# A product-key expert layer in a two-layer diffusion backbone: 75 instead of 80 dense classes, 56 instead of 50 gathered slots per token, nine instead of eight rounds of eight picks

## The chip, the cores and the metric

The kernel runs on one core of a Trainium2 chip, as one program. The metric is device time in microseconds (us) for one execution, from the chip's own profiler or from timed runs; lower is better. Engines are named as in the profile: PE is the matrix engine, PEld its weight loads, DVE the vector engine, ACT the scalar engine, POOL the engine that issues the gathers, SP the one that issues the ordinary loads.

## The reference

A backbone of two layers over 256 tokens of width 1024. Layer 0 mixes with state-space heads and latent attention, layer 1 with a gated MLP. After either mixer comes the part that the change concerns, an expert layer with product keys:

```python
s1 = einsum('thd,hkd->thk', q[..., :half], k1); s2 = einsum('thd,hkd->thk', q[..., half:], k2)
v1, i1 = top_k(s1, 16);  v2, i2 = top_k(s2, 16)               # 8 heads, 128 keys each
top_s, j = top_k(v1 + v2 over all pairs, 16)                  # 16 experts of 16384 per head
gate = softmax(top_s)
act = gelu(einsum('phkd,pd->phk', u_tab[idx], t))             # rows of the u table
out = einsum('phk,phkd->pd', gate * act, v_tab[idx])          # rows of the v table
```

So each token picks 8 x 16 = 128 experts, and each expert is a row of 1024 numbers in the u table and one in the v table, in float32.

## The kernel before

An expert (i1, i2) belongs to class (i1 + i2) mod 128; each of the 128 classes has 128 experts. Classes 0 to X-1 are computed densely, for all 256 tokens, whether they were picked or not. Experts picked from classes X to 127 are gathered, row by row.

**Dense classes.** `products()` issues the PE's work. For each class of a first pass ("S"), eight float32 products of the u weights (a 512 KB load, `in_dn` to a `wr` buffer; there are four) with the tokens `phf` give scores in a `pa` bank; ACT applies gelu and the result lands in row c of the tile `ge`. For each class of a second pass ("V"), eight products of `ge` with the v weights (again 512 KB) accumulate in four `pb` banks, `py`. A float32 product is two records in the profile, so one class is 16 records in either pass.

**Spread.** Between the passes `ge` has to be multiplied with the gates. `spread()` does so in 32 blocks of eight tokens: DVE builds one-hot tiles `o1`, `eq` and `oc` by comparison (their widths hold X), PE multiplies them (16 records of 128x80), DVE and ACT apply the result. The V pass starts when all blocks are done.

**Own slots.** `gather()` works through CAP slots for each of two tiles of 128 tokens (t = 0, 1). A slot holds one gathered expert for each of the 128 tokens: POOL issues one indirect transfer of up to 128 rows of 8 KB (u and v side by side, from `in_uv`) to one of NR = 6 `rows` buffers, DVE takes the dot product with the tokens (`junk<-rows,h`), ACT applies gelu and gate, DVE adds the weighted row to `acc`. A token that has no more picks carries an index out of bounds there, and its row isn't moved. Between t = 0 and t = 1 `acc` is stored (`acs<-acc`) and used again. The indices come out of `take8()`, one round of eight largest keys per call: MAX8, MATCH_REPLACE8, some small operations and eight `mk` operations. There are ROUNDS rounds for each t. Those that the slots of t = 0 and t = 1 don't need at once are drawn one by one in the iterations of t = 1 from its fifth slot on.

**The shared list.** Picks in places CAP to 8 * ROUNDS - 1 go to a list that all tokens share, with room for SHARED * 128 = 384. `listing()` builds it (DVE counts, `cnt`, and small products on PE). Its three slots are gathered last, each with a second gather of the tokens (`rows<-hs`), and DVE makes a tile `sc` of weights; PE then adds them to the same `py` banks (`pb<-rows,sc`, 24 records for three slots). If more picks are left over than the list holds, a branch `overflow()` works them off at the end.

**Order.** Each engine works through its own queue in the order in which the program was written. That order comes from `schedule()`, a planner that runs at build time with its own clocks: it always takes the stream whose engine is least far. Its costs are 3.42 for a class on PE, 2.93 for a row transfer and 1.49 for a class load on one clock "D" for all transfers. `gather()` is held back by a pace:

```python
rest = len(todo) - head[0] + len(work)
nxt[0] = max(nxt[0], clk["T"] - 3.0) + PACE * PTILE * max(0, left[0] - TAIL) / max(1, rest)
if rest:
    yield lambda: clk["T"] > nxt[0] and not urgent()
```

`left` counts the dense classes still to come (both passes), PTILE is 3.5 and TAIL is 10. When the list's `sc` is ready by the planner's clock, its products are written into PE's queue at the place that PE has reached by then; the classes that come later stand behind them. After the last class `update()` adds `py` and `acc` to the stream `x`.

All groups of the profile carry the line 169, that of a helper which every operation passes through, so they are told apart by tiles.

Of the kernel before, what the change touches and what calls it, by code (L numbers as in the profile page):

```python
# [23 lines left out]
EPS = 1e-6  # L24
NEG = -3.0e38

X = 80
GSC = 32768.0
ROOM = 36
TB, TL = 8, 4  # L30
CAP = 50
ROUNDS = 8
SHARED = 3
NR = 6
PRI = {}
# [162 lines left out]
def tile_backbone(ctx: ExitStack, tc: tile.TileContext, a: dict, out: bass.AP):  # L198
# [102 lines left out]
    ms = [dp.tile([P, 512], F32, name=f"ms{g}") for g in (1, 2)]  # L301
    LEFT = 8 * ROUNDS - CAP
    lts = dp.tile([2 * P * LEFT, 2], F32, name="lts")
# [93 lines left out]

    PEER = [(w, c_) for w in "SV" for c_ in range(X)]
    feed = Feed()
# [198 lines left out]
    def hybrid(mod):  # L598
# [444 lines left out]
        def scores():  # L1043
            for p_ in range(4):
# [40 lines left out]
                for h in range(2):  # L1085
                    b0 = 64 * h
                    for t in range(2):
# [4 lines left out]
                        mx = h2.tile([P, 1], F32, tag="mx", name="mx", bufs=4)  # L1092
                        V.tensor_reduce(mx, ps, axis=AX.X, op=ALU.max)
                        V.tensor_scalar(mx, mx, -scale, None, op0=ALU.mult)
# [196 lines left out]
    def gmlp(mod, a1, sh1):  # L1291
# [29 lines left out]
        def centre(t):  # L1321
            mu = gw.tile([P, 1], F32, tag="mu", name="mu")
            V.reduce_sum(mu, sums[t], axis=AX.X)
            V.tensor_scalar(mu, mu, 1.0 / 2048, None, op0=ALU.mult)
            V.tensor_scalar(v[t], v[t], mu, None, op0=ALU.subtract)
            for hf in range(2):
                junk, vh = gw.tile([P, D], F32, tag="xw", name="junk"), v[t][:, hf * D:(hf + 1) * D]
                V.scalar_tensor_tensor(junk, vh, 1.0, vh, op0=ALU.mult, op1=ALU.mult, accum_out=lss[t][:, hf:hf + 1])
            V.reduce_sum(lr[:, t:t + 1], lss[t], axis=AX.X)

# [82 lines left out]
    def peer(l, mod, a2, sh2):  # L1413
# [22 lines left out]
        hh = q1.tile([P, KD, 256], F32R, name="phh", tag="phh")  # L1436
        ge = q1.tile([P, X, 256], F32, name="ge")
        pkT = [q1.tile([P, 4, P], F16, name=f"pkT{t}") for t in range(2)]
        gidx = [q1.tile([P, 8 * ROUNDS], I32, name=f"gidx{t}") for t in range(2)]
        gsel = [q1.tile([P, 8 * ROUNDS], F32, name=f"gsel{t}") for t in range(2)]  # L1440
        gte = [q1.tile([P, P], F32, name=f"gte{t}") for t in range(2)]
# [3 lines left out]
        xb, g2 = spare[1:3], spare[3]  # L1445
        left = [2 * X]
        done = set()
# [150 lines left out]
        def take8(t, r_, idx=None, gsl=None):  # L1598

            if idx is None:  # L1600
                idx, gsl = gidx[t][:, 8 * r_:8 * r_ + 8], gsel[t][:, 8 * r_:8 * r_ + 8]
            ks = q2.tile([P, 8], F32, tag="ks", name="ks")
            V.max(ks, key[t][r_ % 2])
            V.match_replace(key[t][(r_ + 1) % 2], ks, key[t][r_ % 2], 0.0)
            ki = q2.tile([P, 8], I32, tag="ki", name="ki")
            V.tensor_copy(ki, ks)
            z_ = q2.tile([P, 8], F32, tag="z_", name="z_")
            V.tensor_scalar(z_, ks, 0.0, 65536.0, op0=ALU.is_equal, op1=ALU.mult)
            V.tensor_scalar(idx, ki, 8, None, op0=ALU.logical_shift_right)
            V.tensor_tensor(idx, idx, z_, op=ALU.add)  # L1610
            V.tensor_scalar(ki, ki, 255, None, op0=ALU.bitwise_and)
            j1 = q2.tile([P, 8], F32, tag="j1", name="j1")
            V.tensor_copy(j1, ki)
            for s_ in range(8):
                mk = q2.tile([P, P], F32, tag="mk", name="mk")
                V.scalar_tensor_tensor(mk, jp1, j1[:, s_:s_ + 1], gte[t], op0=ALU.is_equal, op1=ALU.mult, accum_out=gsl[:, s_:s_ + 1])
# [192 lines left out]
        def listing():  # L1809
# [4 lines left out]
            for t in range(2):  # L1814
                vm = q2.tile([P, LEFT], F32, tag="vm", name="vm")
                V.tensor_scalar(vm, gidx[t][:, CAP:], 65536.0, None, op0=ALU.is_lt)
                V.reduce_sum(cnt[:, t:t + 1], vm, axis=AX.X)
                V.tensor_copy(rhs[:, t, 1:2], cnt[:, t:t + 1])
                gl = q2.tile([P, LEFT, 2], F32, tag="gl", name="gl")
                V.tensor_copy(gl[:, :, 0], gidx[t][:, CAP:])  # L1820
                V.tensor_copy(gl[:, :, 1], gsel[t][:, CAP:])
                S.dma_start(out=lts[t * P * LEFT:(t + 1) * P * LEFT, :].rearrange("(p j) c -> p (j c)", j=LEFT), in_=gl.rearrange("p j c -> p (j c)"))
                fl = q2.tile([P, 1], F32, tag="fl", name="fl")
                V.tensor_reduce(fl, key[t][ROUNDS % 2], axis=AX.X, op=ALU.max)
                V.tensor_scalar(fl, fl, 0.0, None, op0=ALU.is_gt)
# [36 lines left out]
        def gather():  # L1862
            yield lambda: "sel" in done
            nxt = [clk["T"]]
            todo = [(t, s) for t in range(2) for s in range(CAP)] + [(2, k) for k in range(SHARED)]
            free, work, pend = list(qr["rows"]), [], []
# [31 lines left out]
            def accumulate():  # L1898
# [11 lines left out]
                else:  # L1910
                    V.scalar_tensor_tensor(acc[1], v_, w, acc[1], op0=ALU.mult, op1=ALU.add)
                if t == 0 and s == CAP - 1:
                    Q.dma_start(out=acs, in_=acc[1])
# [7 lines left out]
            while work or pend:  # L1921
                weigh_last()
                if work:
# [6 lines left out]
                    if t == 1 and s >= 4:  # L1930

                        if taken[0] < ROUNDS or taken[1] < ROUNDS:
                            t_ = 0 if taken[0] < ROUNDS else 1
                            take8(t_, taken[t_])
# [196 lines left out]
```

## Time and profile before

| what | value |
|---|---|
| timed runs, median of 3 (lowest to highest) | 2077.2 us (2073.23 to 2078.44) |
| the profiled execution | 2073.34 us, of it span 2071.6 us |
| PE busy | 1945.0 us, 94% of the span |
| DVE busy | 1368.5 us, 66% |
| POOL busy | 592.2 us, 29% |
| HBM read | 525.60 MB, 257 GB/s over the span |
| first V class on PE, layer 0 | 865.0 us |
| first V class on PE, layer 1 | 1747.5 us |

The span is counted from the first to the last instruction; the windows below are us from its start. A busy engine isn't an engine at its peak: a product that waits inside PE's pipeline still counts as busy.

### The profile page before, as it was taken

How to read it: one execution, taken by the hardware profiler on the slowest of the kernel's cores; microseconds unless marked ns; L12 is line 12 of the kernel's file. 1: busy time of each engine (PE TensorE's matmuls, PEld its weight loads, DVE VectorE, ACT ScalarE, POOL GpSimd, SP SyncE). 2: the span in 40 equal slices, each digit the busy share in tenths (PEclk: the TensorE clock that was granted, in tenths of full speed). 3: DMA queues.
4: the chain of work that ended last, by engine and by line, in shares of the span. 5: the costliest groups of instructions: out<-in, count | busy, mean ns of one | idle time of the engine just before them, and what ended most of it. 6: DMA issues, size and time to landing. Idle time of an engine off the chain costs nothing.

```text
span 2071.6 us, 28401 instructions
## 1 busy us (share of the span) xinstructions
PE 1945.0 (94%) x10048; PEld 1574.3 (76%) x10048; DVE 1368.5 (66%) x3634; ACT 540.4 (26%) x1386; POOL 592.2 (29%) x378
## 2 busy tenths in 40 slices
PE   7899999999989999998999998999899999989997
PEld 4565444579878888887877788789688888878786
DVE  3575566247988678878664226579888887776651
ACT  4434343344212122210111154442122221101100
POOL 1324222166011112223221188550111112233210
PEclk9999999999989999999999999999999999989999
DMA  8556664555468668998997364454678788989972
GB/s 302 171 184 215 212 217 145 165 173 184 133 225 293 237 220 310 379 378 293 417 410 260 132 234 153 156 191 128 229 283 307 269 297 298 365 295 412 413 274 82
DMA packets 132489, 519.98 MB, mean 251 GB/s; under 512 B 17222, under 2 KB 17414, under 8 KB 107179
## 3 DMA queue, kind: packets, MB, share of 16 engines
q1 hardware_dynamic: 100320, 312.24, 43.2%
q0 software_dynamic: 30720, 204.69, 25.9%
q8 instruction: 79, 1.29, 0.2%
q10 hardware_dynamic: 1296, 1.15, 0.2%
q14 instruction: 74, 0.61, 0.1%
HBM read 525.60 MB, written 6.91 MB: 257 GB/s over the span
## 4 chain that ended last, share of the span: by engine, by line
PE 55%; DVE 19%; issue 12%; DMA 7%; POOL 5%; ACT 2%; POOLq 0%; SPq 0%; ACTq 0%; DVEq 0%
PE pb L169 28%; PE pa L169 27%; DVE ge L169 6%; DMA wr<-in_dn 4%; POOL rows L169 2%; DVE mk L169 2%; POOL whl L169 2%; DVE acc L169 1%; DVE junk L169 1%; DMA acs<-acc 1%; DVE rows L169 1%; DMA rows<-in_uv,gidx 1%; DVE x L169 1%; DVE oc L169 1%; DVE cacc L169 0%
## 5 line engine op out<-in xcount | busy, mean ns | idle before, releaser
L169 PE MATMUL pa<-phf,wr 128*128 128x256 f32 x2560 | 576.1, 386 | 0.0
L169 PE MATMUL pb<-wr,ge 128*128 128x256 f32 x2560 | 569.4, 383 | 6.5 <-DMA wr<-in_dn 5.4
L169 PEld LDWEIGHTS pb<-wr,ge 128*128 128x128 f32 x2560 | 485.2, 191 | 90.3 <-DMA wr<-in_dn 22.9
L169 PEld LDWEIGHTS pa<-phf,wr 128*128 128x128 f32 x2560 | 492.3, 194 | 67.2
L169 POOL DMA_INDIRECT rows<-in_uv,gidx x200 | 231.7, 1158 | 916.8 <-DVE acc L169 608.0
L169 POOL TENSOR_TENSOR whl<-wr,whl 128x1024 fp32r<-128x1024 f32 (+2 forms) x130 | 314.7, 2434 | 401.9 <-ACT whl L169 392.2
L169 DVE SCALAR_TENSOR_TENSOR junk<-rows,h 128x1024 bf16<-128x1024 f32 x200 | 244.0, 1220 | 85.6 <-DMA rows<-in_uv,gidx 82.5
L169 DVE SCALAR_TENSOR_TENSOR acc<-rows,wt,acc 128x1024 f32<-128x1024 f32 x196 | 250.7, 1279 | 0.0
L169 ACT ACTIVATE act<-act 128x1 f32<-128x1 f32 x206 | 41.7, 203 | 435.6 <-DVE junk L169 420.6
L169 ACT CAST whl<-wr 128x1024 fp32r<-128x1024 f32 (+2 forms) x136 | 136.9, 1018 | 70.7 <-PE pa L169 27.7
L169 ACT ACTIVATE sg<-pa 128x256 f32<-128x256 f32 (+25 forms) x126 | 38.8, 308 | 383.9 <-PE pa L169 375.4
L169 PE MATMUL pb<-oc,o 128*128 128x80 f16 x1024 | 88.2, 255 | 31.8 <-DVE oc L169 31.8
L169 PEld LDWEIGHTS <-o 128*128 128x128 f16 x1024 | 80.8, 118 | 40.9 <-DVE o L169 16.3
L169 PE MATMUL pa<-phh,whl 128*128 128x256 f32 x512 | 96.3, 285 | 2.1 <-DVE phf L169 2.1
L169 PE MATMUL pb<-aw,condT 128*32 128x512 f32 x328 | 93.4, 624 | 5.1 <-DVE mod L169 3.0
L169 DVE SCALAR_TENSOR_TENSOR ge<-pb,ge 128x80 f32<-128x80 f32 (+29 forms) x128 | 36.9, 316 | 78.3 <-ACT ge L169 77.2
L169 PEld LDWEIGHTS pa<-phh,whl 128*128 128x128 f32 x512 | 80.8, 191 | 4.0 <-DVE phf L169 2.5
L169 PE MATMUL pa<-phl,whl 128*128 128x256 f32 x256 | 73.2, 286 | 2.4 <-POOL phl L169 1.3
L169 DVE SCALAR_TENSOR_TENSOR mk<-jp,j,gte 128x128 f32<-128x128 f32 x256 | 72.4, 347 | 1.1
L169 PE MATMUL pb<-whl,cath 128*128 128x512 f32 x192 | 61.8, 400 | 2.0 <-POOL whl L169 1.1
L169 ACT ACTIVATE wt<-act,gsel 128x1 f32<-128x1 f32 x200 | 58.9, 295 | 6.5
L169 DVE TENSOR_TENSOR oc<-eq,pkT 128x640 f16<-128x640 f16 x128 | 57.1, 487 | 2.2
(517 smaller groups left out, 2402.0 us busy)
## 6 DMA issues: line engine op xcount, KB each, us to landing
wr<-in_dn SPq DMA_DIRECT2D x320, 512.0 KB
aw<-in_ada_w SPq DMA_DIRECT2D x164, 256.0 KB
wr<-in_wq SPq DMA_DIRECT2D x32, 512.0 KB
wr<-in_w_out SPq DMA_DIRECT2D x16, 512.0 KB
wr<-in_gm_w_v SPq DMA_DIRECT2D x16, 512.0 KB
wr<-in_gm_w_u SPq DMA_DIRECT2D x16, 512.0 KB
wr<-in_gm_w_out SPq DMA_DIRECT2D x16, 512.0 KB
wr<-in_w_xbc SPq DMA_DIRECT2D x12, 512.0 KB
```

What stands on the lines that cost most here:

```text
L169: return f(*args, **kw)
```

## The change

Three constants. X sets how many classes are dense, and with it the length of both passes, the size of `ge`, the width of the spread's tiles and the split of the tables in memory. CAP is the number of own slots per token tile; ROUNDS is the number of calls of `take8()` per token tile. The room for the list's candidates per token, 8 * ROUNDS - CAP, goes from 14 to 16.

```diff
-X = 80
+X = 75
 GSC = 32768.0
 ROOM = 36
 TB, TL = 8, 4
-CAP = 50
-ROUNDS = 8
+CAP = 56
+ROUNDS = 9
 SHARED = 3
 NR = 6
```

## Rows read from the trace of the kernel before

**Rows 1.** From the page: the span; the gathers' queue (packets, MB, share).
```profile
span 2071.6 us, 28401 instructions
...
q0 software_dynamic: 30720, 204.69, 25.9%
```

**Rows 2.** Windows by stage: us, busy by engine (instructions), PE clock, DMA share, GB/s.
```profile
606.00:864.00 258.00, 250.44 (x1425) 220.61 (x1423) 200.30 (x472) 54.01 (x239) 41.60 (x40) 0.97 0.77 281
864.00:960.00 96.00, 86.08 (x397) 74.32 (x395) 83.58 (x319) 11.08 (x43) 28.42 (x19) 0.97 0.92 352
960.00:1000.00 40.00, 40.00 (x187) 35.46 (x186) 26.34 (x53) 4.97 (x20) 17.00 (x13) 0.93 0.89 329
1000.00:1100.00 100.00, 98.39 (x438) 81.23 (x437) 67.13 (x84) 13.93 (x56) 26.69 (x27) 1.00 1.00 404
...
1121.00:1176.00 55.00, 55.00 (x250) 43.68 (x249) 5.14 (x11) 4.29 (x9) 0.00 (x0) 1.00 0.37 124
...
1490.00:1754.00 264.00, 255.34 (x1487) 226.20 (x1488) 217.48 (x518) 57.63 (x260) 47.82 (x45) 0.97 0.82 297
...
1876.00:1976.00 100.00, 97.78 (x429) 79.25 (x428) 64.08 (x81) 12.93 (x52) 25.70 (x26) 1.00 1.01 410
```

**Rows 3.** Timeline of PE, end of layer 0: start, us, what.
```profile
1099.77 30.38 PE L169 MATMUL pb<-wr,ge 128*128 128x256 f32 x140
1129.99 10.46 PE L169 MATMUL pb<-rows,sc 128*128 128x512 f32 x24
1140.29 34.70 PE L169 MATMUL pb<-wr,ge 128*128 128x256 f32 x160
```

**Rows 4.** Timeline of DVE, end of layer 0; in brackets idle time before it.
```profile
1109.08 0.41 DVE L169 TENSOR_SCALAR sc<-iotaL,spot,wt 128x256 f32<-128x256 f32 x1
...
1120.84 0.08 DVE L169 DVE_READ_ACCUMULATOR junk<-rows,rows 128x1 f32 x1
1133.70 0.41 DVE L169 TENSOR_SCALAR sc<-iotaL,spot,wt 128x256 f32<-128x256 f32 x1 [12.78 <-PE pb L169]
...
1170.71 0.69 DVE L169 TENSOR_TENSOR x<-pb,ge 128x512 f32<-128x512 f32 x1 [36.30 <-PE pb L169]
```

**Rows 5.** Timeline of PE, end of layer 1.
```profile
2015.09 10.46 PE L169 MATMUL pb<-rows,sc 128*128 128x512 f32 x24
2025.39 34.70 PE L169 MATMUL pb<-wr,ge 128*128 128x256 f32 x160
```

**Rows 6.** Timeline of DVE, end of layer 1.
```profile
2006.29 0.08 DVE L169 DVE_READ_ACCUMULATOR junk<-rows,rows 128x1 f32 x1
```

**Rows 7.** Groups of 1000 to 1100: count, busy us, mean ns, idle before it.
```profile
L169 PE MATMUL pb<-wr,ge 128*128 128x256 f32 x438 | 99.0, 383 | 1.6 <-DMA wr<-in_dn 1.1
...
L169 DVE SCALAR_TENSOR_TENSOR acc<-rows,wt,acc 128x1024 f32<-128x1024 f32 x28 | 35.8, 1279 | 0.0
L169 DVE SCALAR_TENSOR_TENSOR junk<-rows,h 128x1024 bf16<-128x1024 f32 x28 | 34.3, 1225 | 34.2 <-DMA rows<-in_uv,gidx 34.2
```

**Rows 8.** The chain that ended last, 960 to 1060: start, us, what.
```profile
968.76 41.56 PE pb L169 x192
...
1036.84 3.72 PE pb L169 x16
```

**Rows 9.** Timeline of PE, the building of the list in layer 0.
```profile
959.45 0.56 PE L169 MATMUL pa<-cnt,tri 128*128 128x1 f32 x2 [7.45 <-DVE cnt L169]
```

**Rows 10.** Groups of 606 to 864, the S stage of layer 0.
```profile
L169 DVE SCALAR_TENSOR_TENSOR junk<-rows,h 128x1024 bf16<-128x1024 f32 x43 | 52.4, 1218 | 0.0
...
L169 DVE TENSOR_TENSOR oc<-eq,pkT 128x640 f16<-128x640 f16 x60 | 26.8, 487 | 1.0
```

**Rows 11.** Timeline of DVE: the first row is the first of a round of picks.
```profile
909.99 0.28 DVE L169 MAX8 ks<-key 128x8 f32<-128x128 f32 x1
...
913.81 1.28 DVE L169 SCALAR_TENSOR_TENSOR acc<-rows,wt,acc 128x1024 f32<-128x1024 f32 x1
```

**Rows 12.** Transfers of 864 to 1120.
```profile
DMA packets 19562, 94.40 MB, mean 369 GB/s; under 512 B 3268, under 2 KB 3268, under 8 KB 12835
```

## The prediction, made before the change was run

> **What bounds the kernel now.** I read the windows by stage first, then the ends of both layers on PE and DVE, then the saturated stretch in between. In the S stage (606 to 864) PE is busy 250 of 258 us, DVE 200, the transfers 77% [rows 2]: PE sets the pace. In the V stage the transfers fill up: 404 GB/s at a share of 1.00 from 1000 to 1100, 410 in layer 1 [rows 2]; there DVE waits 34.2 of 100 us for gathered rows [rows 7], and PE's classes come every 100 / (438 / 16) = 3.65 us [rows 7] instead of 41.56 / 12 = 3.46 [rows 8]. So after 864 the gathers run at the transfers' limit and PE just behind its own.
>
> The reader should look longest at the end of a layer. PE meets the list's products at 1129.99, and behind them stand 160 records, ten classes, 34.70 us [rows 3]; layer 1 is the same [rows 5]. DVE has the list ready just before: first `sc` at 1109.08, third dot product finished at 1120.84 (layer 1: 2006.29); its third `sc` then waits 12.78 us only because PE hasn't used the first [rows 4, 6]. After that DVE idles 36.30 us for PE [rows 4]. The 55 us from 1121 on with transfers at 37% [rows 2] look like ample cover for more gathers. They aren't: PE works its queue in order, and a list that comes after PE has reached its place holds back every class behind it. The true slack is 1130 - 1121 = 9 us, and this decides the change.
>
> **What the change removes.** Five S and five V classes in each layer: 10 x 3.46 = 34.6 us of PE a layer, 69.2 in all [rows 8]. Were PE alone the bound, that would be the gain. The one-hot tiles get 6% narrower: `oc` takes 487 ns for 640 elements [rows 10], and if all of it scaled, 64 of them would save 2 us of DVE a layer; bounds 0 and 5 with `eq` and the applying; it falls into the S stage, where DVE idles 58 of 258 us [rows 2], so I take 0. PE's spread products get narrower as well; 0 too.
>
> **What it adds.** Two layers of two tiles get six more own slots: 24 gathers, 12 a layer, each 1.225 + 1.279 = 2.50 us of DVE [rows 7], 30 us a layer. Two more rounds of picks a layer at 913.81 - 909.99 = 3.82 us [rows 11]: 7.6. They come in the burst behind the store of `acc`, where DVE is busy 83.6 of 96 us [rows 2] and nothing hides them: everything behind them on DVE's queue, the building of the list and all later slots, moves by 7.6.
>
> Transfers: I counted the reference's own picks for these inputs. Classes from 80 on get 48.3 and 48.0 picks a token in the two layers, from 75 on 53.3 and 53.0. Own slots then move 13335 rows instead of 11978 in layer 0 (13332 and 11990 in layer 1), the list 306 instead of 376 (230 and 301). In bytes up to the list's end: +1357 x 8192 = 11.1 MB, -70 x 12288 = -0.9, and ten class loads fewer at 0.524, -5.2: together +5.0 MB. (By this count the old gathers move (11978 + 11990) x 8192 + 677 x 12288 = 204.7 MB, which the page's queue shows [rows 1].) At the V stage's mean of 369 GB/s [rows 12] 5.0 MB are 13.6 us.
>
> So the list is ready later than before, in absolute time, by 0 us if the S stage takes all of it (23% of its transfer time is idle [rows 2]), by 12 x 100 / 28 = 42.9 plus 7.6 = 50 us if each new slot costs what a slot costs in the saturated stretch [rows 7]. I take the bytes and the picks, 13.6 + 7.6 = 21.2: the stage behind S is limited by bytes most of the time [rows 2], the burst by DVE. That the S stage ends 17 us sooner gives the gathers nothing: they are ordered by the same queue and filled its holes before.
>
> The Trainium skill's page "DMA: Bandwidth & Descriptors" (Specifications) gives about 358 GB/s as the limit of one core's memory traffic. The rows contradict it here, with 404 and 410 [rows 2]. By it the 107 MB of the new V stage (94.4 [rows 12], 13 more gathers of 0.98 there) would need 299 us from 848, the list would come at 1148 and not at 1142, and the total would be some 12 us higher.
>
> **Where the list stands in PE's queue.** The planner deals out about one gather per class in V: its transfer clock is full with 2.93 + 1.49 = 4.42 per pair, more than PE's 3.42. Before, 43 of the first 50 slots are done by 864 [rows 10]: 57 own and 3 list slots are left, the eight rounds of picks cost it some ten more classes, and it ends with ten classes left, where TAIL wants it. After, S gives about as many slots (five classes shorter, DVE-limited in the planner's order): 70 + 3 slots and ten rounds against 75 classes. One by one that is more than there are; the pace, 3.5 x (75 - 10) / 73 = 3.1 at the start and shorter after the burst, lets it catch up in part. Bounds: no class behind the list and ten; I take four.
>
> **The sum, layer 0.** PE reaches the list at about 848 + 71 x 3.65 + 12 for building the list (its 7.45 us wait [rows 9] and the products) = 1119. The first `sc` comes at 1109.1 + 21.2 = 1130, the third dot at 1142.0. Then 0.4 for `sc`, 10.46 / 3 = 3.5 for the last products [rows 3], 4 x 3.47 = 13.9 for the classes behind, and 2.8 for the clock: after the 7.45 us wait it is granted 0.93 over 40 us [rows 2], that is 2.8 us lost at the lower level. End at 1162.6 instead of 1140.29 + 34.70 = 1175.0: 12.4 us less. Layer 1: 2006.3 + 21.2 + 20.6 = 2048.1 instead of 2060.1, 12.0 less. Together -24.4. The profiled execution took 2073.3 (span 2071.6 and 1.7 around it): 2048.9. The median of the runs is 3.9 above the profiled one, so I predict 2053.
>
> **The rivals.**
> *PE keeps the end.* The S stage swallows the slots, or the list stands at the very end. The full 34.6 a layer less about 4 for more classes at 3.65 rather than 3.46: -61, 2016; with the list last and ready at 1142, 1149 a layer, 2025. For it: DVE's and the transfers' holes in S. Against it: gathers in S are tied to the pace of the classes, of which there are fewer. Chance 0.17, 2010 to 2030.
> *The list holds ten classes back,* the other side. One mechanism: it still stands ten classes before the end, as in both layers now [rows 3, 5], and PE, 29 us earlier there, waits. End = ready + 3.9 + 34.7 + 2.8; it decides from ready = 1133.6 on, against 1120.84 now. With 1142: 1183.4, +8.4 a layer, 2094; with four classes but every slot at its saturated price (ready 1171), 1192, 2111. For it: both layers agree on ten, and TAIL aims there. Against it: one gather per class isn't enough for it. Chance 0.17, 2084 to 2115.
> *Nothing comes of it,* 2071 to 2083: between these, for instance eight classes behind, or the limit of 358 GB/s with six. Chance 0.14.
> *More than the classes' own time:* under 2010, the narrower spread counting as well: 0.02.
> *The branch for picks left over runs.* It would cost hundreds of us, but the count excludes it: 306 and 230 left over against 384 places, and the largest token has 70 picks against 72. No chance.
>
> **How the numbers follow.** The forecast, 2030 to 2070, has 0.50. With half of the first rival, the no-change case and a good part of the slow one, 2020 to 2095 holds about 0.8. A difference of 0.3% (6 us, 2071 to 2083) is about what a measurement tells from none: faster 0.17 + 0.50 + 0.02 = 0.69, same 0.14, slower 0.17.
>
> **What would show it.** The profile after should have PE waiting 15 to 25 us in each layer before `pb<-rows,sc`, released by DVE's `sc`, where it didn't wait before; about 64 records of classes behind the list instead of 160; DVE's 36.30 us wait for PE shrunk to some 15; the last dot at 1142 and near 2026 less what layer 0 gained; 224 own gathers and 225 MB on their queue; 20 classes fewer. If PE doesn't wait there, the first rival holds. The prediction is wrong if the list's place moves less than I think, or if the S stage takes up more slots: each slot more done there is worth 3.6 us a layer.

## The result and the profile after

The changed kernel takes 2043.6 us (median of four runs, 2037.8 to 2047.3) against 2077.8 before: ratio 0.984 [0.982, 0.986], or 33 us less. The forecast was 2053, range 2020 to 2095, so direction and range held. The changed kernel's profiled execution took 2042.83 us, its span 2041.0 (2071.6 before). Times "against the changed kernel" below are differences of ratios to the kernel before, times 2077.

The page of the changed kernel, the lines that answer to [rows 1]:
```profile
span 2041.0 us, 28033 instructions
...
PE 1886.9 (92%) x9728; PEld 1516.0 (74%) x9728; DVE 1429.6 (70%) x3796; ACT 545.9 (27%) x1438; POOL 630.8 (31%) x402
...
q0 software_dynamic: 34176, 225.07, 29.1%
```
225.07 MB on the gathers' queue is what the count of picks gave. PE is busy 58.1 us less (1945.0 before), less than the 69.2 that twenty classes take.

PE's timeline at the end of layer 0 of the changed kernel:
```profile
1137.25 12.71 PE L169 MATMUL pb<-rows,sc 128*128 128x512 f32 x24 [9.50 <-DVE sc L169]
1149.80 10.52 PE L169 MATMUL pb<-wr,ge 128*128 128x256 f32 x48
```
And at the end of layer 1:
```profile
2004.13 8.83 PE L169 MATMUL pb<-rows,sc 128*128 128x512 f32 x16 [2.18 <-DVE sc L169]
2013.48 3.70 PE L169 MATMUL pb<-rows,sc 128*128 128x512 f32 x8 [0.52 <-DVE sc L169]
2017.02 13.98 PE L169 MATMUL pb<-wr,ge 128*128 128x256 f32 x64
```
Three and four classes now stand behind the list where there were ten [rows 3, 5], and PE waits for `sc`, which it did not before: 9.5 us in layer 0, 2.7 in layer 1. The Trainium skill's page "PSUM — Partial Sum Buffer" (Engine vs sequencer instructions) says that products start and finish in the order in which they were issued. The trace agrees: the 48 records behind the list need only their weights and `ge`, and start at 1149.80, behind the list's products.

DVE's timeline there:
```profile
1090.52 1.23 DVE L169 SCALAR_TENSOR_TENSOR junk<-rows,h 128x1024 bf16<-128x1024 f32 x1 [1.04 <-DMA rows<-in_uv,gidx]
...
1125.23 1.22 DVE L169 SCALAR_TENSOR_TENSOR junk<-rows,h 128x1024 bf16<-128x1024 f32 x1
...
1127.57 1.22 DVE L169 SCALAR_TENSOR_TENSOR junk<-rows,h 128x1024 bf16<-128x1024 f32 x1
...
1136.79 0.41 DVE L169 TENSOR_SCALAR sc<-iotaL,spot,wt 128x256 f32<-128x256 f32 x1
...
1145.12 0.08 DVE L169 DVE_READ_ACCUMULATOR junk<-rows,rows 128x1 f32 x1
...
1156.05 0.69 DVE L169 TENSOR_TENSOR x<-pb,ge 128x512 f32<-128x512 f32 x1 [9.55 <-PE pb L169]
```
The row at 1090.52 is the 100th own slot; the same slot was the last one before, at 1100.52. The 112th is at 1127.57. The last three come 2.34 us apart without a wait for rows: at the end DVE sets their pace.

PE's rows at the building of the list, layers 0 and 1:
```profile
972.82 0.56 PE L169 MATMUL pa<-cnt,tri 128*128 128x1 f32 x2 [13.69 <-DVE cnt L169]
...
1842.80 0.56 PE L169 MATMUL pa<-cnt,tri 128*128 128x1 f32 x2 [14.32 <-DVE cnt L169]
```
This wait was 7.45 us [rows 9] and 8.8 in layer 1. Ahead of the building PE has 31 and 30 V classes in its queue where it had 24 in both layers. DVE's counts are there 450.4 and 446.5 us after the layer's first S product where they took 439.3 and 431.4, that is 11 and 15 later. The windows of the changed kernel (columns as in [rows 2]): S stage with the spread, V stage, the stretch that holds this wait, the saturated stretch:
```profile
522.00:841.00 319.00, 305.10 (x1725) 268.49 (x1724) 273.03 (x807) 67.37 (x277) 48.90 (x44) 0.97 0.74 262
841.00:1160.00 319.00, 287.74 (x1256) 238.78 (x1254) 232.96 (x569) 41.57 (x159) 94.87 (x77) 0.95 0.89 345
960.00:1000.00 40.00, 27.18 (x120) 24.05 (x121) 30.45 (x107) 3.98 (x16) 15.65 (x11) 0.79 0.74 250
1000.00:1100.00 100.00, 99.00 (x437) 80.85 (x436) 66.05 (x82) 13.43 (x54) 28.20 (x27) 1.00 1.02 417
```
The two stages before:
```profile
520.00:865.00 345.00, 327.97 (x1803) 288.07 (x1802) 282.75 (x816) 71.58 (x277) 50.09 (x46) 0.96 0.71 255
865.00:1175.00 310.00, 298.47 (x1339) 251.40 (x1339) 192.36 (x477) 34.81 (x132) 76.98 (x63) 0.98 0.85 324
```
The reader should see that in layer 0 the whole gain lies in S, 345 to 319. The V stage lost five classes, 17.3 us, and still grew from 310 to 319. Layer 1 is alike: S from 338 to 321, V from 313 to 314. PE's waits from 480 to 1180, from the view of waits (total, times, longest):
```profile
PE pa L169 <- DVE cnt L169: 13.7, 1, 13.7
PE pb L169 <- DVE oc L169: 12.3, 5, 8.6
PE pb L169 <- DVE sc L169: 9.5, 1, 9.5
PE pb L169 <- DMA wr<-in_dn: 7.1, 1, 7.1
```

Before, the wait for class loads (`wr`) was 3.6 and that for `oc` 16.7. These waits and those of layer 1 go into the sum at the end.

For the experiments the same stages in one table, in us of each profiled execution: S from the first S product to the first V product, V from there to the last product of either kind, by the starts and ends of PE's timeline; PE's waits for `oc` in S; and all its waits in V, with those at the building and at the list in brackets.

| kernel | S, layer 0; 1 | waits for `oc` | V, layer 0; 1 | waits in V, layer 0; 1 (building, list) |
|---|---|---|---|---|
| before | 344.9; 338.0 | 16.7; 15.0 | 310.0; 312.6 | 11.0 (7.4, 0); 10.6 (8.8, 0) |
| changed | 318.8; 320.6 | 12.3; 14.5 | 319.2; 314.3 | 30.3 (13.7, 9.5); 22.8 (15.8, 2.7) |
| e1 dense only | 328.1; 326.6 | 19.0; 16.5 | 301.9; 294.7 | 13.4 (5.3, 3.3); 9.3 (5.5, 0) |
| e2 slots only | 340.0; 346.4 | 14.1; 15.9 | 309.7; 312.3 | 8.3 (5.2, 0); 11.1 (10.1, 0) |
| e3 list last | 318.8; 320.2 | 12.3; 14.8 | 314.7; 306.6 | 23.8 (11.5, 3.2); 19.8 (15.8, 0) |
| e4 own acc | 318.8; 319.2 | 12.1; 14.3 | 305.6; 315.7 | 15.7 (4.5, 5.1); 25.4 (12.6, 7.7) |
| e5 late building | 319.0; 311.3 | 12.3; 10.4 | 314.1; 307.4 | 24.8 (10.8, 5.3); 19.2 (10.9, 3.3) |
| e8 all three | 318.8; 311.3 | 12.4; 9.8 | 298.7; 302.0 | 12.0 (1.8, 5.3); 15.2 (6.1, 0) |
| e9 dense, all three | 328.1; 323.6 | 18.7; 16.8 | 288.6; 289.9 | 6.8 (5.7, 0); 5.7 (5.7, 0) |
| e10 before, two edits | 343.8; 348.1 | 16.8; 19.8 | 305.8; 310.3 | 6.1 (2.8, 0); 8.1 (4.9, 0) |
| e12 changed, two edits | 318.9; 318.3 | 12.3; 12.8 | 307.3; 305.9 | 21.5 (11.2, 0.7); 20.3 (9.7, 0) |

### The profile page after: what moved, and what is told of

It is laid out like the page before. It is cut to its first block, busy times and chain, and to the rows that moved or that the text cites. A ratio compares the mean times of both kernels' runs of the same rounds, so it can differ in the third digit from the quotient of the medians.

```text
span 2041.0 us, 28033 instructions
## 1 busy us (share of the span) xinstructions
PE 1886.9 (92%) x9728; PEld 1516.0 (74%) x9728; DVE 1429.6 (70%) x3796; ACT 545.9 (27%) x1438; POOL 630.8 (31%) x402
## 3 DMA queue, kind: packets, MB, share of 16 engines
q0 software_dynamic: 34176, 225.07, 29.1%
## 4 chain that ended last, share of the span: by engine, by line
PE 36%; issue 29%; DVE 17%; POOL 12%; ACT 2%; DMA 2%; POOLq 0%; SPq 0%; ACTq 0%; DVEq 0%
PE pa L169 23%; PE pb L169 14%; POOL rows L169 10%; DVE ge L169 6%; POOL whl L169 2%; DVE rows L169 1%; DVE acc L169 1%; DMA rows<-hs,lidx 1%; DVE oc L169 1%; DVE junk L169 1%; DVE mk L169 1%; DVE x L169 1%; DVE o L169 1%; DVE cacc L169 0%; POOLq L169 0%
## 5 line engine op out<-in xcount | busy, mean ns | idle before, releaser
L169 POOL DMA_INDIRECT rows<-in_uv,gidx x224 | 266.8, 1191 | 930.0 <-DVE acc L169 619.9
L169 PE MATMUL pb<-wr,ge 128*128 128x256 f32 x2400 | 542.1, 386 | 13.1 <-DMA wr<-in_dn 11.3
L169 PE MATMUL pa<-phf,wr 128*128 128x256 f32 x2400 | 539.8, 385 | 0.0
L169 PEld LDWEIGHTS pb<-wr,ge 128*128 128x128 f32 x2400 | 458.5, 193 | 96.5 <-DMA wr<-in_dn 32.1
L169 PEld LDWEIGHTS pa<-phf,wr 128*128 128x128 f32 x2400 | 459.8, 193 | 62.0
L169 POOL TENSOR_TENSOR whl<-wr,whl 128x1024 fp32r<-128x1024 f32 (+2 forms) x130 | 314.7, 2434 | 363.6 <-ACT whl L169 337.4
L169 DVE SCALAR_TENSOR_TENSOR junk<-rows,h 128x1024 bf16<-128x1024 f32 x224 | 273.5, 1221 | 99.9 <-DMA rows<-in_uv,gidx 99.7
L169 DVE SCALAR_TENSOR_TENSOR acc<-rows,wt,acc 128x1024 f32<-128x1024 f32 x220 | 281.8, 1281 | 0.0
L169 PE MATMUL pb<-oc,o 128*128 128x75 f16 x1024 | 85.3, 252 | 28.6 <-DVE oc L169 26.8
L169 PEld LDWEIGHTS <-o 128*128 128x128 f16 x1024 | 78.2, 118 | 38.0 <-DVE o L169 16.5
L169 DVE SCALAR_TENSOR_TENSOR ge<-pb,ge 128x80 f32<-128x80 f32 (+31 forms) x128 | 37.0, 323 | 73.4 <-ACT ge L169 73.2
L169 ACT ACTIVATE ge<-pa 128x256 f32<-128x256 f32 (+24 forms) x136 | 40.2, 296 | 81.4 <-PE pa L169 81.4
```

Of the source, the lines that this page charges most:

```text
L169: return f(*args, **kw)
```

## The experiments

The edits are shown shortened, that of e7 against the kernel before, the others against the changed one.

**e1, the dense classes alone.** 75 classes, but slots and rounds as before; the picks of classes 75 to 79 are skipped.
```diff
-CAP, ROUNDS = 56, 9
+CAP, ROUNDS = 50, 8
-V.tensor_scalar(mk, cls, float(X), None, op0=ALU.is_ge)
+V.tensor_scalar(mk, cls, 80.0, None, op0=ALU.is_ge)
```


> 75 dense classes, but 50 slots and eight rounds as before; picks of classes 75 to 79 are left out altogether, so the gathers have exactly the work they had before. In this program's order the list stands seven classes before the end in both layers. Theory (the list and its place set the end): the gathers have no reason to be earlier than before, the third dot comes near 1121 in layer 0, PE waits for it, and the end is 1121 + 4 + 7 x 3.47 + about 3, that is 23 to 26 us a layer: 2026 to 2031. Rival (PE's own work sets the end): the whole 34.6 us of ten classes a layer, 2008 to 2016.


Measured 2019.7, ratio 0.973 [0.969, 0.977], -56 us: between the two theories. PE's timeline in layer 0 shows the list's mechanism, a wait of 3.02 for the last `sc` and seven classes behind it:
```profile
1122.74 5.40 PE L169 MATMUL pb<-rows,sc 128*128 128x512 f32 x8 [3.02 <-DVE sc L169]
1127.98 24.34 PE L169 MATMUL pb<-wr,ge 128*128 128x256 f32 x112
```
The layer ends 22.7 us sooner; layer 1, where PE did not wait for the list, gains 29.3.

**e2, the slots and rounds alone,** at 80 classes.
```diff
-X = 75
+X = 80
```


> 80 dense classes with 56 slots and nine rounds; result unchanged. The list stands six and seven classes before the end. Bytes hardly change (337 rows of 8 KB more in slots, 337 list rows of 12 KB fewer in layer 0), DVE gets 30 + 7.6 us a layer more. If the gathers are limited by bytes, the list is ready 7.6 later, at 1128, before PE gets there near 1153, and only the longer wait for building the list remains, some 6 us a layer: 2086 to 2092. If each slot has its price in DVE time whatever it moves, the list is ready near 1158 and PE waits as well: 2092 to 2105. Together with the run of 75 classes alone it should add up to the change's -34.


Measured 2075.6, 0.999 [0.998, 1.001]: nothing, so both losses that were expected stayed away, though the list really is later. DVE's first `sc` and PE's list and last classes:
```profile
1136.04 0.41 DVE L169 TENSOR_SCALAR sc<-iotaL,spot,wt 128x256 f32<-128x256 f32 x1
```
```profile
1142.60 10.46 PE L169 MATMUL pb<-rows,sc 128*128 128x512 f32 x24
1152.89 20.88 PE L169 MATMUL pb<-wr,ge 128*128 128x256 f32 x96
```
`sc` is 27 us later than in [rows 4], but the planner put the list four classes further back (six behind it; seven in layer 1), and PE came after `sc` was ready. So -56 and 0 do not add up to -33: the slots cost time only together with the fewer classes. By the table that is in V: from e1 to the changed kernel it grows by 17.3 and 19.6, from the kernel before to e2 by nothing.

**e7, the rounds alone:** the kernel before with one more round of picks for each token tile.
```diff
-ROUNDS = 8
+ROUNDS = 9
```


> The kernel before with nine instead of eight rounds of picks, still 50 slots and 80 classes; result unchanged. Theory (a round is 3.8 us on DVE's chain, PE notices it only where it waits for DVE): two rounds a layer, the list ready 7.6 later, at 1117 to 1128, still ahead of PE near 1130; PE's wait for building the list 7.4 and 8.8 grows by a few us in each layer: 0 to +8, 2076 to 2085. Rival (the rounds alone explain the longer waits at the building, 13.7 and 14.3): +10 to +14.


Measured 0.999 [0.998, 1.000]. The first `sc` came at 1112.76 instead of 1109.08, 4.1 us later from the layer's start (5.7 in layer 1), not 7.6. DVE's counts for the list, though, come 12 and 15 us later from there, as much as in the changed kernel: a round is drawn in the iteration of a slot, so two more rounds put two more slots ahead of the counts as well (64 instead of 62). PE's wait there did not grow by that, because the planner wrote the building four and three classes further back; PE's row in layer 0:
```profile
970.97 0.39 PE L169 MATMUL pa<-cnt,tri 128*128 128x1 f32 x2 [4.04 <-DVE cnt L169]
```

**e6, the bytes alone:** the changed kernel, in which slots 50 and up move only rows with index 0, so that their transfers carry next to nothing.
```diff
-fetch(bufs[0], gidx[t][:, s:s + 1])
+fetch(bufs[0], gidx[t][:, s:s + 1], last=0 if s >= 50 else (P - X) * P - 1)
```


> The changed kernel, with every operation of the slots 50 to 55 kept, but their transfers given a bound that lets no row through (their picks are left out of the result): some 806 rows, 6.6 MB, a layer less. If the new slots cost bytes, as the prediction has it, the list is ready 18 us sooner in each layer (second weights of the list near 1123 instead of 1140.8), PE's waits for it vanish: -12 to -16, 2028 to 2032. If they cost DVE's time and the round trip of a slot whatever it moves: the list at 1137 to 1141 as now, 0 to -4, 2040 to 2044.


Measured 0.978 [0.977, 0.980], 12 us under the changed kernel. The first and second `sc` of layer 0:
```profile
1133.51 0.41 DVE L169 TENSOR_SCALAR sc<-iotaL,spot,wt 128x256 f32<-128x256 f32 x1
...
1138.50 0.41 DVE L169 TENSOR_SCALAR sc<-iotaL,spot,wt 128x256 f32<-128x256 f32 x1
```
That is 3.3 and 2.3 sooner than in the changed kernel, 5 to 6 from the layer's own start (2.8 later here), and some 3 in layer 1. By the prediction's price of a byte it should have been 18. The time follows neither theory alone: the median fell as far as the theory of bytes has it, while in the profiled executions, 6.9 apart, the layers end 5.5 and 2.8 sooner from their first S products. The windows of the changed kernel and of e6 around the last own slots show what was taken away:
```profile
1095.00:1127.00 32.00, 31.94 (x149) 27.60 (x148) 25.12 (x33) 5.44 (x22) 11.55 (x10) 1.00 0.96 366
```
```profile
1095.00:1125.00 30.00, 30.00 (x140) 25.94 (x140) 26.21 (x34) 5.48 (x22) 13.54 (x11) 1.00 0.76 278
```
The transfers' share falls from 0.96 to 0.76, but each of these slots still takes DVE 2.34 us.

**e3, the list last.** Three ways of taking the waits from PE follow. First, the changed kernel with the list's products held back until all classes are in PE's queue.
```diff
 if pend[0][0] == 2:
+    yield lambda: "pl" in done
```


> The changed kernel, with the list's products written behind the last class in PE's queue; nothing else. Theory: the last third of the list is ready at 1145.8 in layer 0 and 2013.4 in layer 1, the classes no longer wait behind it; layer 0 ends at 1149.5 instead of 1160.3, layer 1 about 4.5 earlier: -15, 2026 to 2031. Rival (the place of the list is of no importance, since PE's own waits for it are small): 0 to -3, 2040 to 2045. Another: the list holds its six row buffers until PE is done, which delays nothing, as no slot comes after it.


Measured 0.979 [0.976, 0.982], 11 us under the changed kernel: the time is as the theory has it, but V is 4.5 and 7.7 shorter, where the theory had 11 and 4.5. The wait for `sc` falls from 9.5 to 3.2 and from 2.7 to nothing.

**e4, an accumulator for each token tile,** so that DVE need not wait until `acc` is stored (6.5 us in layer 0 of the changed kernel).
```diff
+acc = [q1.tile([P, D], F32, name=f"acc{t}") for t in range(2)]
-if t == 0 and s == CAP - 1: Q.dma_start(out=acs, in_=acc[1])
-if t == 0: Q.dma_start(out=acc[0], in_=acs)
```


> The changed kernel with a sum tile of its own for each token tile, so that the sum isn't stored and loaded again and DVE doesn't wait 6.5 and about 11 us for the store. In this order the list moves to the very end in layer 0 and to five classes before it in layer 1. Theory (DVE's chain of slots and picks sets both of PE's waits, for building the list and for the list): both get shorter by the wait taken away, 13.7 and 14.3 at the building by 6 to 11, the list's 9.5 and 2.7 wholly: -20 to -28, 2016 to 2024. Rival (behind that point the transfers limit the gathers, so the time is only spent waiting for rows instead): 0 to -6, 2037 to 2044.


Measured 0.976 [0.973, 0.980], 16 us under the changed kernel, less than expected: the waits at the building shrank to 4.5 in layer 0 but to 12.6 only in layer 1, where the wait for the list rose to 7.7 and V did not get shorter.

**e5, the building of the list later in PE's queue:** DVE's counts are issued where they were, PE's products four slots later.
```diff
+for _ in range(4):
+    yield
 for t in range(2):
     mm(ps[:, t:t + 1], tri, cnt[:, t:t + 1], True, t == 0)
```


> The changed kernel; PE's small products that build the list are written four slots later into PE's queue, so that DVE's counts are there when PE comes to them; the list then stands two classes before the end in both layers. If the ready list alone sets the end, PE gets to it 14 us sooner and waits 14 longer, and what is left is one or two classes fewer behind the list: -3 to -8, 2036 to 2041. If PE's own time sets it, its waits of 13.7 and 14.3 us at the building are gained: -20 to -28, 2016 to 2024.


Measured 0.973 [0.971, 0.976], 22 us under the changed kernel; the slots and the list carry the same work as there. By the table V is 5.1 and 6.9 shorter, its waits 5.5 and 3.6; the other 9.3 are a shorter S stage of layer 1, where PE waits 4.1 less for `oc`: the edit does not touch that stage, but the planner now places its spread otherwise among the classes. So of the 20 to 28 expected from V only 12 came from there. Part of the building's wait came back one step later, now for a product with `cmp` while ACT is still at `wt`:
```profile
991.05 2.69 PE L169 MATMUL pa<-rhs,cmp 128*128 128x2 f32 x12 [10.79 <-ACT wt L169]
```

**e8, all three edits on the changed kernel.**

> The changed kernel with the list last, a sum tile for each token tile and the late building of the list. Theory (PE's waits for DVE in the V stage are what the change lost, 28 us at the building and 12 at the list, and the three edits take most of them away): 25 to 32 us below the changed kernel, 2011 to 2019. Rival (the gathers' chain itself is the bound and PE only waits elsewhere): as with the list last or the own sum alone, 2026 to 2031.


Measured 2005.3, 0.966 [0.964, 0.968]: 71 us under the kernel before, 38 under the changed one, the fastest of all. PE's waits in V fall from 53.1 to 27.2 in both layers together, V itself by 32.8, as the theory has it; the gain beyond that is S of layer 1, 9.3 shorter as in e5. PE's timeline, layers 0 and 1:
```profile
1121.52 12.61 PE L169 MATMUL pb<-rows,sc 128*128 128x512 f32 x24 [5.26 <-DVE sc L169]
...
1974.28 10.46 PE L169 MATMUL pb<-rows,sc 128*128 128x512 f32 x24
```

**e9, the three edits with dense classes alone** (e1 and e8 together; the picks of 75 to 79 are skipped).

> The three edits of the fastest version so far (list last, own sums, late building), with 75 dense classes but 50 slots and eight rounds; picks of classes 75 to 79 are left out. It stands to that version (2005.3) as 75 classes alone (2019.7) stood to the changed kernel (2043.6), where slots and picks cost 24 us. Theory (slots and picks cost PE only through its waits for DVE, which the edits take away): 2000 to 2006, no or a few us faster. Rival (they have a price of their own): 20 to 26 faster, 1979 to 1985.


Measured 2008.4, 0.966 [0.964, 0.968], the same as e8. With the waits moved, 24 slots and four rounds cost nothing in the sum, which is what the theory said. But not for its reason: in V they cost 10.1 and 12.1 us by the table, and S is 9.3 and 12.3 shorter with them, where PE waits 6.3 and 7.0 less for `oc`.

**e10 and e12, late building and list last** on the kernel before (e10) and on the changed one (e12). Is the gain of the edits the change's, or the edits' alone?

> The kernel before (80 classes, 50 slots, eight rounds) with the list last and its late building; result unchanged. With 80 classes PE waits 7.4 and 8.8 us at the building and not at all for the list: -10 to -16, 2061 to 2068, if PE's own time is the bound there. If the list or the gathers bound it, nothing: 2074 to 2079.

> The changed kernel with the list last and its late building, the counterpart of the run before with 80 classes. Late building alone gave 2022.4, the list last alone 2029.8; as the waits for the list that are left are small, 2015 to 2022. Against the same edits at 80 classes the five classes should then be worth 45 to 50 us, more than the 33 that they brought without the edits; if they bring 33 again, the waits were not what the change lost.


e10 measured 1.003 [1.001, 1.004], a miss: a gain was expected. V got 4.2 and 2.3 us shorter, but the S stage of layer 1 ten longer, with 4.8 more of waiting for `oc`. DVE shows that the edit itself took hold: with the list at the end, the wait for PE to use the first `sc` grew from 12.78 to
```profile
1164.63 0.41 DVE L169 TENSOR_SCALAR sc<-iotaL,spot,wt 128x256 f32<-128x256 f32 x1 [43.76 <-PE pb L169]
```
e12 measured 0.971 [0.969, 0.974], 27 us under the changed kernel. Between e10 and e12 lie 0.0314, 65 us, close to the 69.2 of twenty classes, but for another reason than I had: S gives 24.9 and 29.8 of it (ten through e10's long S of layer 1), V next to nothing, since PE still waits 21.5 and 20.3 us there in e12 against 6.1 and 8.1. So there late products still cost V its five classes; in e8, where the accumulator's edit brings DVE forward as well, V is 8.6 and 3.9 shorter.

**e11, a step further:** 70 classes, 61 slots, ten rounds, the three edits.
```diff
-X, CAP, ROUNDS = 75, 56, 9
+X, CAP, ROUNDS = 70, 61, 10
```


> One step further with the three edits: 70 dense classes, 61 slots, ten rounds; result unchanged. PE loses ten more classes a layer, 69 us in all; ten more slots and two more rounds a layer put the list some 23 us later, by the measured 27 for twelve slots and two rounds. In the version with 75 PE waits 5 us for the list in layer 0 and none in layer 1, so with 70 the list sets the end of both: about 1130 + 23 - 17 for the earlier end of the pass before, at best. Theory: 2000 to 2030, no gain or a loss. Rival (PE still the bound): 1940 to 1960.


Measured 0.974 [0.971, 0.977], 17 us slower than e8. In layer 1 the list bounds, though it stands last:
```profile
1989.76 8.69 PE L169 MATMUL pb<-rows,sc 128*128 128x512 f32 x16 [18.94 <-DVE sc L169]
```
In layer 0 it does not: PE waits 3.6 us for it, and V is 8.6 shorter than in e8. There S is 9.2 longer, though it has five classes fewer, since PE's waits for `oc` grow from 12.4 to 30.9 (from 9.8 to 22.2 in layer 1).

## Why the prediction was right, and where it was not

*The list's place and the end of the layer: right.* Four classes behind the list were forecast, three and four stand there. In layer 0: third dot product 1145.2 against 1142.0; last product 1160.3 against 1162.6; -14.7 us in layer 0 and -14.4 in layer 1 by the timelines, against -12.4 and -12.0. PE waits for `sc`, and DVE's last wait for PE falls from 36.30 to 9.55 in layer 0 (some 15 forecast). e3 confirms it from the other side: with nothing behind the list, 11 us come back.

*The 21.2 us by which the list comes later: right in size by luck, wrong in both parts.* The third dot is 24.3 later in absolute time in layer 0, some 20 in layer 1 from that layer's start. I had put it as 13.6 for bytes and 7.6 for two rounds. By e6 a byte costs a sixth to a third of what I took, and e7 leaves 4 to 6 for the rounds. Two steps of opposite sign make up the rest. "The S stage ends 17 us sooner gives the gathers nothing" failed: the 50th slot comes at 870 instead of 887 and the 100th at 1090.5 instead of 1100.5, two more rounds included (in layer 1 18 us sooner from the first slot on). With 75 classes and the old slots (e1) the 50th comes at 882, with 80 classes and the new ones (e2) at 872, so most of it is not the shorter stage. In the planner's code the pace divides by `rest`, and more slots to do would release each one sooner; no run tries this by itself. Against that, the twelve new slots took 1127.6 - 1090.5 = 37 us, 3.1 each, between DVE's own pace (2.50 by the sum of [rows 7], 2.34 at the end, where its records overlap) and the 3.6 of the saturated stretch. 37 - 10 is the 27 us by which the last slot moved. So each new slot had to be paid for, as in my upper bound, and the earlier start that I had ruled out took part of it back: two errors that cancelled.

*"12 for building the list", taken unchanged: the step that failed.* The building waits for DVE's counts. The prediction itself moved them by 7.6 and let PE come sooner, and yet it kept the wait of 7.45. The counts came 11 and 15 us later, which e7 shows to be the rounds and the slots that are drawn with them. PE, with five S classes fewer and seven or six V classes more ahead of the building, came only 4.8 and 9.6 later, and the wait went from 7.45 to 13.7 and from 8.8 to 14.3 (15.8 with a short one behind it). Neither half of the change does as much alone: the wait is 5.3 and 5.5 in e1, 5.2 and 10.1 in e2. So PE came to the list at 1127.75 and not at 1119, and waited there 9.5 and 2.7 instead of 15 to 25. Part of the delay had been paid before it got there. e5 shows the cost.

*Where 69 us of classes went.* The sum had S 17 us shorter and, from 848 to 1162.6, V some 5 longer than its 310. In layer 0 S gave 26.1 and V grew by 9.2, two misses that cancel; in layer 1 it was 17.4 and 1.7. The traces account for all four. The lower clock is counted as half of the time that PE's clock was granted at the lower of its two levels (1.2 instead of 2.4 GHz), outside of PE's waits:

| us, changed less before | S, layer 0; 1 | V, layer 0; 1 | sum |
|---|---|---|---|
| five classes | -17.3; -17.3 | -17.3; -17.3 | -69.2 |
| PE's waits | -3.8; -0.4 | +19.3; +12.2 | +27.3 |
| the lower clock | -3.5; +2.3 | +5.5; +6.0 | +10.3 |
| the rest | -1.5; -2.0 | +1.7; +0.8 | -1.0 |
| measured | -26.1; -17.4 | +9.2; +1.7 | -32.6 |

(The spans differ by 30.6, mostly because layer 0's first S product comes 2 us later in the changed kernel's execution.) So 31.5 us of new waits in V and 11.5 of the lower clock beside them took gain back, while S gave 9 beyond its classes. That the waits are the cause is shown by e3 and e4 (V 4.5 and 7.7 shorter when the list stands last; 13.6 shorter in layer 0 of e4, where most of the building's wait goes and the list stands last too) and by e8. That the lower clock comes of the waits is argued from where it stands, behind them; no run isolates it.

*The rivals.* That PE keeps the end came true only in kernels whose late products stand elsewhere: e12, where PE hardly waits for the list, measured 2019.6, within that rival's 2010 to 2030, and e8 lies below it. The list that holds ten classes back did not come: the planner moved it, in e2 too. Nor did the time stay what it was. In the second rival, PE would have reached its list 33 us earlier by the sum's own figures (848 + 65 x 3.65 + 12 = 1097), not 29; nothing else in it uses this.

*The limit of 358 GB/s* that the prediction took from the Trainium skill and weighed would have made it 12 us more. The stretch from 1000 to 1100 ran at 417. The Trainium skill's page "HBM Reference" (Specifications (TRN2)) gives about 425 for a core that streams alone, which is this case; the trace, with 404 to 417, agrees.

*What moves S.* S of layer 1 moves by some 10 us with no edit in it: 346 and 348 in e2 and e10 against 338 at 80 classes, 311 in e5 and e8 against 319 to 321 at 75. Counted as in the table above, it is waits and the lower clock: +4.8 and +4.1 of e10's 10.1, -4.2 and -5.7 of e5's 9.3, +1.3 and +7.5 of e2's 8.4. PE's timelines show why it is not chance. Where two kernels have each of the 32 blocks of the spread behind the same class, S is the same within 2 us: 318.7 to 319.0 in layer 0 of the changed kernel, e3 to e6, e8 and e12; 343.8 to 344.9 in that of the kernel before, e7 and e10; 328.1 to 328.2 in that of e1 and e9. In layer 1 the changed kernel, e3, e4 and e6 share one order (319.2 to 320.8), e5 and e8 another (311.3), the kernel before and e7 a third (338.0 and 340.1); e2 and e10 have orders of their own. So the 9 us that S gave beyond its classes, and the shorter S with more slots in e8 beside e9, come with the order in which the planner put the spread.

*Open.* What in an order makes PE wait more or less for `oc` was not tried. The first S product of layer 0, too, comes anywhere from 516.7 to 525.6 in the profiled executions. Both limit what e5, e9, e10 and e12 say of a few us.

## What to carry to other kernels

Slack at the end of a stage isn't cover: measure, for each product that waits for another engine, how long before PE's place its input is ready, since all work behind it in PE's queue waits too. A saving on the bounding engine brings that engine sooner to every such place, so go through all of them (here the list and its building), and move them back before judging the change. Price an added slot from the stretch in which it will run, and ask separately whether its start moves and what else is drawn along with it.

## What the runs showed of the hardware

A wait of PE cost more here than its length. The first two windows are the 20 us behind the 13.7 us wait of the changed kernel, the other two those behind the 7.45 us wait of the kernel before:
```profile
972.80:982.80 10.00, 9.98 (x39) 8.82 (x39) 6.57 (x26) 0.99 (x4) 2.15 (x2) 0.59 0.65 213
982.80:992.80 10.00, 10.00 (x50) 8.86 (x50) 5.14 (x12) 1.00 (x4) 6.13 (x5) 1.00 0.73 236
```
```profile
959.45:969.45 10.00, 10.00 (x46) 9.12 (x47) 6.66 (x26) 1.00 (x4) 2.15 (x2) 0.71 0.76 239
969.45:979.45 10.00, 10.00 (x48) 8.81 (x47) 4.42 (x13) 0.99 (x4) 6.12 (x5) 1.00 0.75 253
```
The clock is granted at 0.59 and 0.71 and then in full, so 4.1 and 2.9 us are lost behind the waits. The class that PE does there takes 6.29 and 5.09 us instead of 3.47. The 0.79 over 960 to 1000 is lower than 0.93 before [rows 2] mostly because that stretch holds the 13.7 us wait itself, and the other one begins just behind its wait.

A share of 1.02 and 417 GB/s over 1000 to 1100 look like a limit set by bytes. e6 does not test that, since the slots that it empties lie almost wholly outside this stretch, which runs at 1.02 and 417 there too. What e6 shows is the floor of a slot: with next to no rows to move it still takes 2.34 us of DVE.
